# The last two units of each output layer taken one token half at a time, with short chains moved and given priority

## The chip, the cores and the metric

The kernel runs on one core of one Trainium2 chip. The metric is the device time of one execution in microseconds (us), the median of several runs. Five compute engines work side by side, each on its own queue of instructions in a fixed order: PE (TensorE) multiplies matrices and transposes, DVE (VectorE) and ACT (ScalarE) do elementwise work and read the PSUM banks that PE fills, POOL (GpSimd) does a little elementwise work, SP (SyncE) issues DMAs. An instruction that waits holds up everything behind it on its own engine.

## The reference

One token sequence (256 tokens of width 1024, fp32) passes through two blocks of a language model. A matrix product is written `@`:

```
first block : x += rms(rwkv_and_conv(rms(x)) @ w_out) * g1      ("wout")
              x += rms(memory_attention(rms(x)) @ wo) * g3      ("wo")
              x += rms(swiglu(rms(x))) * g5                     (FFN wgu, wdn)
second block: x += swiglu(rms(x))       f1, layer 0
              x += attention(rms(x)) @ wao      (rotary positions, 8 heads)
              x += swiglu(rms(x))       f2, layer 0
              x += swiglu(rms(x))       f1, layer 1
              x += ssm(rms(x)) @ wso            (8 groups of 4 heads)
              x += swiglu(rms(x))       f2, layer 1
swiglu(h) = (silu(h @ Wg) * (h @ Wu)) @ Wd, 2816 = 11 * 256 wide
```

The first three sums normalise the product before it is added to x (the change's texts call this "with post"); the six of the second block add it as it is ("without post").

## The kernel before

**Precision.** Every operand of a large product is split into a high and a low part, and a product is three matmuls: high by high, high by low, low by high. For activations the split comes with the eviction from PSUM: ACT writes the high part, then DVE the low part out of the same bank and the high part (L383 and L384 after a transpose; L301 and L303 elsewhere).

**Weights.** `unit()` brings 1 MB of weights by DMA, ACT casts it in two halves to `wh` (L205, L198), and DVE subtracts to get `wl` (L207, L199); for some units of the SSM stage POOL does this subtraction instead. `wh` and `wl` have four half-unit buffers each, so a cast waits until PE has done with the half four back.

**Products.** An FFN has 11 chunks c: gate and up products of chunk c, four transposes of chunk c-1, and the down product of chunk c-1 into four PSUM banks `acc` (two token halves th by two column halves o). `down_steps` runs a down unit over all four banks; only for the last unit of a layer it goes bank by bank, and `fin.done(th, o)` is called when a bank is complete. The layers wout, wo, wao and wso use the same function.

**Between layers.** `Fin.done` adds the finished bank to x. Without post that is one DVE sum (L414). With post ACT squares the bank and sums (L426), DVE and POOL make the root (L430, L317, L318), and DVE scales and adds (L436, L437). Then `square` sums x squared on ACT (L370) for the next layer's norm, and `PreT.turn(th, q)` transposes four 128x128 blocks of x on PE (L378) and evicts each block by ACT (L383) and DVE (L384): these blocks are the next layer's operand, k = 4q to 4q+3. The next layer's first chunk c0 takes token half 0 through k = 0 to 7 before half 1, so that it needs the turns of half 1 later ("late" turns, taken after an odd k).

**Order.** PE runs in the order in which the program is written. `weave()` mixes a list of generators of large products with short chains, each started at a given step and moved on by what it yields, so that a product step stands between two links of a chain. DVE, ACT and POOL are ordered by a scheduler that goes by readiness and by the priority of the code (`tc.high_priority()`).

**Attention.** `pair(j)` norms and rotates two heads (`rope_norm`, L1176 to L1194), and E0 steps later transposes them (`to_F`, L1201). **SSM.** `steps()` makes the step sizes by a softplus chain of some twenty 128x64 operations (L1339 to L1367, last the tile `adt`). `group(g)` starts every eight steps: ACT turns two banks of broadcast sums into decays (L1440), DVE makes the conv (L1402, L131), masks (L1452), PE mixes, DVE collects y (L1490 to L1493), ACT squares (L1496), POOL takes a power (L1499), DVE multiplies 2 numbers per lane (L1500), ACT scales (L1502), and D2 steps later PE transposes y (L1507).

Of the kernel before, what the change touches and what calls it, by code (L numbers as in the profile page):

```python
# [97 lines left out]
def _build(ctx, nc, tc, a):  # L98
# [176 lines left out]
    def down_steps(acc, u, yf, first, fin=None, every=2):  # L275

        hh, hl = yf()
        if fin is not None:
            for th in range(2):
                for o in range(2):  # L280
                    for k in range(2):
                        down_part(acc, u, hh, hl, th, o, k, first, True)
                    fin.done(th, o)
                    yield
            return
# [77 lines left out]
    class PreT:  # L363
# [8 lines left out]
        def turn(self, xt, th, q):  # L372
# [8 lines left out]
            for i in range(4):  # L381
                k, b = 4 * q + i, bk[:, i * 128:i * 128 + 128]
                S.mul(self.xh[:, k, t], b, pc(gname, gi + k))  # L383
                V.scalar_tensor_tensor(self.xl[:, k, t], b, pc(gname, gi + k), f(self.xh[:, k, t]), MUL, SUB)  # L384
# [7 lines left out]
    class Fin:  # L392
# [10 lines left out]
        def turn(self, th, q):  # L403
            self.nxt.turn(self.xt, th, q)

        def turns(self, *w):
            for th, q in w:
                self.late.append(lambda th=th, q=q: self.turn(th, q))

        def done(self, th, o):  # L410
            xt, c = self.xt, slice(o * 512, o * 512 + 512)
            x, y = xt[:, th, c], flat(self.acc[2 * th + o])
            if self.post is None:
                V.tensor_tensor(x, x, y, ADD)  # L414
# [17 lines left out]
            for o in range(2):  # L432
# [5 lines left out]
                self.nxt.square(th, o, x)  # L438
            self.turns((th, 0), (th, 1))
# [371 lines left out]
    y_c = []  # L811
# [89 lines left out]
    def mem_v_unit(j, u, pool, late):  # L901
        mh_, ml_, rbm, rm = kv["x"]
        bk = bank(pool)
        for k in range(8):
            linT_step(bk, u, mh_, ml_, k)
            if k == 3:
                late.pop(0)()
                late.pop(0)()
# [5 lines left out]
    def wout_units():  # L914
        acc.extend([bank(psa), bank(psa), bank(psa), bank(psf)])
        for j, y in enumerate([y_r[0], *y_c]):
            hl = split(y)
            yield from down_steps(acc, unit(a["wout"][(2, 0, 1)[j]]), lambda: hl, j == 0, None, 1)
# [19 lines left out]
    order.__enter__()  # L938
    yl = split(y_r[1])
    u = unit(a["wout"][3])  # L940
# [4 lines left out]
    run(down_steps(acc, u, lambda: yl, False, fin))  # L945
    mem_v_unit(3, um, psb, fin.late)
    for t in fin.late:
        t()
    mixing.close()
    psa = mkpool("psa", 4, space=PSUM)  # L950

# [60 lines left out]
    def outs_():  # L1012
        acc.extend(new_acc())
        for h in range(4):
            u = unit(a["wo"][h], True)
            if h == 3:
                nf.extend(two("wgu", 0)())
                fins.append(Fin(xt, acc, nxt2, "g3r"))
            yield from down_steps(acc, u, lambda: oh[h], h == 0, fins[0] if h == 3 else None)

    fill = [first_heads()]
    for h in (2, 3):
        fill.append(pieces(lambda h=h: unit(a["wq"][h], True), qb[h]))
    fill.append(outs_())
    weave(fill, [(8, mem_head(0)), (9, mem_head(1)), (11, mem_head(2)), (15, mem_head(3))])

    def rope_tables():
# [39 lines left out]
        tab = {}  # L1067
        for n in ("qn", "kn"):
# [6 lines left out]
            tab[n] = (cg, sg_)  # L1075
        return tab


    def ffn(wgu, wd, l, pre, nf, late, nxt, post=None, ahead=None):

        acc = new_acc()
        late = list(late)
        while len(late) > 2:
            late.pop(0)()
# [18 lines left out]

        for c in range(11):
            us = nf if c == 0 else (unit(a[wgu][l * 22 + 2 * c], True, ahead=True), unit(a[wgu][l * 22 + 2 * c + 1], True))
            b = bank(), bank()
            if c in (0, 10):
                for th in range(2):
                    for k in range(8):
                        wide_step(b, us, xh, xl, k, (th,))  # L1110
                        if k % 2 and late:
                            late.pop(0)()
                        if c and th == 0 and k == 5:
                            hl = turned(c - 1)
                    if c == 0 and th == 0:
# [6 lines left out]
            else:  # L1122
# [4 lines left out]
                for th in range(2):  # L1127
                    evict(c, b[th], th)
            d = unit(a[wd][l * 11 + c], True)
            if c:  # L1130
                for i, _ in enumerate(down_steps(acc, pend, lambda: hl, c == 1)):
                    if c == 10 and i == 1:
                        hl10 = turned(10)
            pend = d
        nf = ahead() if ahead else None
        fin = Fin(xt, acc, nxt, post)
        run(down_steps(acc, pend, lambda: hl10, False, fin))
        return nf, fin.late

    rope = rope_tables()  # L1140
    pre, late = nxt2, fins[0].late
    nx = PreT("f1", 0)
    nf, late = ffn("wgu", "wdn", 0, pre, nf, late, nx, "g5r", two("f1gu", 0))
    pre, nx = nx, PreT("mx", 0)
    nf, late = ffn("f1gu", "f1d", 0, pre, nf, late, nx, None,
# [7 lines left out]
    late_ = list(late)  # L1153
# [16 lines left out]
    def rope_norm(bks, n):  # L1170
        r, r2 = norm
        ss = small(8)
        s4 = ss.rearrange("p (h q) -> p h q", h=2)
        for h, bk in enumerate(bks):
            sq = s2("n")
            S.activation(sq, bk, AF.Square)  # L1176
            V.tensor_reduce(s4[:, h], v3(sq), AX.X, ADD)
        V.tensor_tensor(s4, s4, blast(r2, 4), MUL)
        V.tensor_scalar(ss, ss, 1.0 / 128, 1e-6, MUL, ADD)
# [454 lines left out]
```

## Time and profile before

| | |
|---|---|
| median of 3 runs (range) | 1663.1 us (1663.08 to 1664.25) |
| the profiled execution | 1663.16 us |
| its span in the trace | 1661.1 us |
| busy: PE, DVE, ACT, POOL | 1600.0, 1058.9, 864.0, 142.9 us |
| mean TensorE clock granted | 0.987 of full |

The span is what lies between the first and the last instruction; some 2.1 us of the time lie around it. PE is busy for 96% of the span. The clock is granted at one of two levels, 2.4 GHz (1.00 in the rows) or 1.2 GHz; a row of a window gives the mean over the window. All busy times are of this one execution.

### The profile page before, as it was taken

The numbers are of one execution on the slowest core, as the hardware profiler recorded it, in microseconds if no ns is written. First come the engines' busy times: TensorE is split into PE (matmuls) and PEld (weight loads), VectorE is DVE, ScalarE is ACT, GpSimd is POOL, SyncE is SP. The second block draws the span as 40 slices with busy tenths as digits, with TensorE's granted clock in tenths as the row PEclk, the third lists the DMA queues.
The fourth block names the chain that finished last, engine by engine and source line by source line (L and its number), as shares of the span: only waits on it lengthen the run. The fifth ranks groups of instructions, "written<-read, shape, count | busy, mean of one in ns | idle before, by whom it ended". The sixth has DMA issues, their size and how long they took to land.

```text
span 1661.1 us, 21983 instructions
## 1 busy us (share of the span) xinstructions
PE 1600.0 (96%) x8702; PEld 1376.1 (83%) x8702; DVE 1058.9 (64%) x1652; ACT 864.0 (52%) x1432; POOL 142.9 (9%) x154
## 2 busy tenths in 40 slices
PE   8999998989999999999999999999999999999999
PEld 7898988878887888877778887888889889778887
DVE  6888855574545554567665556555559999665453
ACT  6734445563445444456664445444456766564442
POOL 2322200000000000000000000000014333000000
PEclk9999999989999999999999999999999999999999
DMA  7321234445454445452345554554533323455451
GB/s 280 133 76 53 88 131 149 150 147 213 165 217 157 159 181 200 172 193 92 140 191 200 179 193 175 188 201 170 195 121 129 151 102 127 150 206 194 186 188 66
DMA packets 39848, 265.99 MB, mean 160 GB/s; under 512 B 4673, under 2 KB 5441, under 8 KB 8385
## 3 DMA queue, kind: packets, MB, share of 16 engines
q1 hardware_dynamic: 39456, 263.41, 43.0%
q8 instruction: 68, 1.11, 0.3%
q10 hardware_dynamic: 288, 1.18, 0.2%
q14 instruction: 36, 0.29, 0.1%
HBM read 263.52 MB, written 1.05 MB: 159 GB/s over the span
## 4 chain that ended last, share of the span: by engine, by line
PE 77%; DVE 13%; ACT 6%; issue 3%; POOL 1%; DMA 0%; SPq 0%; POOLq 0%; ACTq 0%; DVEq 0%
PE bk L181 74%; DVE wl L207 3%; PE bk L1101 1%; ACT wh L205 1%; DVE s2w L1427 1%; DVE cv L131 1%; DVE s2w L131 1%; DVE sm L1500 1%; ACT s2w L1405 1%; ACT s2w L1440 1%; PE bk L740 1%; ACT s2n L370 0%; PE bk L378 0%; ACT s L383 0%; DVE s2w L436 0%
## 5 line engine op out<-in xcount | busy, mean ns | idle before, releaser
L181 PE MATMUL bk<-wh,s 128*128 128x512 f32 (+1 forms) x2400 | 735.6, 381 | 10.2 <-DVE s L384 4.8
L207 DVE TENSOR_TENSOR wl<-raw,wh 128x1024 fp32r<-128x1024 f32 x344 | 420.2, 1227 | 266.0 <-ACT wh L205 264.3
L205 ACT CAST wh<-raw 128x1024 fp32r<-128x1024 f32 x366 | 382.0, 1049 | 291.2 <-PE bk L181 278.9
L181 PEld LDWEIGHTS bk<-wh,s 128*128 128x128 f32 x2400 | 441.3, 190 | 94.4 <-DVE s L384 8.2
L181 PE MATMUL bk<-wl,s 128*128 128x512 f32 (+1 forms) x1200 | 449.8, 375 | 0.0
L181 PE MATMUL bk<-wh,s2f 128*128 128x512 f32 x1072 | 344.6, 392 | 0.0
L181 PEld LDWEIGHTS bk<-wl,s 128*128 128x128 f32 x1200 | 228.0, 190 | 37.0
L181 PEld LDWEIGHTS bk<-wh,s2f 128*128 128x128 f32 x1072 | 201.3, 188 | 41.6 <-issue 0.2
L181 PE MATMUL bk<-s,wh 128*128 128x256 f32 x1120 | 220.2, 296 | 8.7 <-ACT wh L528 5.9
L181 PE MATMUL bk<-wl,s2f 128*128 128x512 f32 x536 | 208.6, 389 | 0.0
L181 PEld LDWEIGHTS bk<-s,wh 128*128 128x128 f32 x1120 | 180.7, 197 | 12.8 <-ACT wh L528 5.9
L199 DVE TENSOR_TENSOR wl<-raw,wh 128x1024 fp32r<-128x1024 f32 x120 | 144.4, 1221 | 66.1 <-ACT wh L198 66.1
L181 PE MATMUL bk<-s,wl 128*128 128x256 f32 x560 | 160.3, 289 | 0.5 <-DVE wl L529 0.4
L198 ACT CAST wh<-raw 128x1024 fp32r<-128x1024 f32 x120 | 123.0, 1051 | 60.2 <-DMA raw<-f1gu 20.6
L303 DVE TENSOR_TENSOR s2f<-bk,s2f 128x512 fp32r<-128x512 f32 x59 | 40.8, 691 | 134.0 <-ACT s2f L301 133.9
L301 ACT CAST s2f<-bk 128x512 fp32r<-128x512 f32 x59 | 34.6, 586 | 171.2 <-PE bk L1101 168.9
L181 PEld LDWEIGHTS bk<-wl,s2f 128*128 128x128 f32 x536 | 100.7, 188 | 20.4
L181 PEld LDWEIGHTS bk<-s,wl 128*128 128x128 f32 x560 | 110.3, 197 | 1.3 <-DVE wl L529 0.9
L318 POOL TENSOR_TENSOR sm<-sm,mh 128x2 f32<-128x2 f32 (+1 forms) x17 | 17.1, 1003 | 775.0 <-DVE sm L317 346.8
L1094 ACT ACTIVATE s2w<-bk,sm 128x256 f32<-128x256 f32 x110 | 50.6, 472 | 36.2 <-PE bk L181 35.7
L1095 DVE SCALAR_TENSOR_TENSOR s2w<-bk,sm,s2w 128x256 f32<-128x256 f32 x110 | 51.9, 482 | 18.6 <-ACT s2w L1094 18.3
L207 POOL TENSOR_TENSOR wl<-raw,wh 128x1024 fp32r<-128x1024 f32 x22 | 54.9, 2499 | 68.3 <-ACT wh L205 68.2
(327 smaller groups left out, 1426.5 us busy)
## 6 DMA issues: line engine op xcount, KB each, us to landing
raw<-f1gu SPq DMA_DIRECT2D x44, 1024.0 KB, 4.8
raw<-f2gu SPq DMA_DIRECT2D x44, 1024.0 KB, 4.8
raw<-wgu SPq DMA_DIRECT2D x22, 1024.0 KB, 4.8
raw<-f1d SPq DMA_DIRECT2D x22, 1024.0 KB, 4.8
raw<-f2d SPq DMA_DIRECT2D x22, 1024.0 KB, 5.2
raw<-wxbc SPq DMA_DIRECT2D x16, 1024.0 KB, 4.8
raw<-wdn SPq DMA_DIRECT2D x11, 1024.0 KB, 6.4
raw<-win SPq DMA_DIRECT2D x10, 1024.0 KB, 4.8
```

The source lines that it names most:

```text
L131: V.scalar_tensor_tensor(o, src, w, o, MUL, ADD)
L181: PE.matmul(out, lhsT, rhs, start=start, stop=stop, skip_group_check=True)
L198: S.copy(h[:, c], r[:, c])
L199: V.tensor_tensor(l[:, c], r[:, c], f(h[:, c]), SUB)
L205: S.copy(h, r[:, c])
L207: (eng or V).tensor_tensor(l, r[:, c], f(h), SUB)
L301: S.copy(hh, src)
L303: V.tensor_tensor(hl, src, f(hh), SUB)
L318: G.tensor_tensor(r, r, mh[:, 0:n], POW)
L740: PE.transpose(bx[:, u], Z[:, u], ident)
L1094: S.activation(t, b[:, 0], AF.Silu, scale=r[:, th:th + 1])
L1095: V.scalar_tensor_tensor(t, b[:, 1], ru[:, th:th + 1], t, MUL, MUL)
```

## The change

- `down_two` is new: the last two units u and v of each output layer run u half 0, v half 0, u half 1, v half 1. The sum into x (and with post the chain before it) of half 0 comes after v half 0. Without post the two turns of half 0 stand between u half 1 and v half 1; with post they stand inside v half 1.
- The sum, and the evictions in `turn`, run at high priority; `square` moves from the sum to the end of `turn`.
- In an FFN the gate and up units of chunk 10 are requested one chunk earlier, and chunk 10 is transposed in two halves (`turned_last`).
- `rope_tables` runs inside the `wo` layer's weave instead of after it.
- `rope_norm` and the softplus chain run at high priority; E0 goes from 5 to 7, D2 from 9 to 11; `group` yields `1 + pr` in place of 1, `weigh` yields 7 or 8 in place of 3 or 4 for the last two.
- The multiply at L1500 moves from DVE to POOL.

```diff
+    def down_two(acc, u, yu, v, yv, fin):
+        for th in range(2):
+            hh, hl = yu(th)
+            for o in range(2):
+                for k in range(2):
+                    down_part(acc, u, hh, hl, th, o, k, False, False)
+            yield
+            if th and fin.post is None:
+                fin.turn(0, 0)
+                fin.turn(0, 1)
+            hh, hl = yv(th)
+            for o in range(2):
+                for k in range(2):
+                    down_part(acc, v, hh, hl, th, o, k, False, True)
+                fin.done(th, o)
+                if th and fin.post is not None:
+                    fin.turn(0, o)
+                yield
...
+            with tc.high_priority():
+                for i in range(4):
+                    k, b = 4 * q + i, bk[:, i * 128:i * 128 + 128]
+                    S.mul(self.xh[:, k, t], b, pc(gname, gi + k))
+                    V.scalar_tensor_tensor(self.xl[:, k, t], b, pc(gname, gi + k), f(self.xh[:, k, t]), MUL, SUB)
+            self.square(th, q, xt[:, th, q * 512:q * 512 + 512])
...
         def done(self, th, o):
+            with tc.high_priority():
+                self.update(th, o)
+            if th:
+                self.late.append(lambda: self.turn(1, o))
...
-            yield 1
+            yield 1 + pr
...
-        V.tensor_tensor(rs, rs, rh, MUL)
+        G.tensor_tensor(rs, rs, rh, MUL)
...
-    D0, D1, D2 = 2, 5, 9
+    D0, D1, D2 = 2, 5, 11
...
-    E0, E1, E2 = 5, 3, 6
+    E0, E1, E2 = 7, 3, 6
```

Two places show how the order moves. The first is ACT at the boundary from FFN f2 of layer 0 to f1 of layer 1. Before: `bk_8694` holds blocks k = 0 to 3 of token half 0 and `bk_8716` blocks 4 to 7, `wh_8824` and `wh_8828` are the halves of the first down unit of the next FFN.

```order
L383 ACTIVATE s8_8692<-bk_8694,pk_121 128x128 [waits PE_49]
L370 ACTIVATE s2n_8690,sm_7375<-s8_2753 128x512 [waits DVE_49]
L383 ACTIVATE s8_8692<-bk_8694,pk_121 128x128 [waits DVE_49]
L205 CAST wh_8824<-raw_8822 128x1024 [waits DMAHW1_49,PE_49,Activation_49]
L383 ACTIVATE s8_8692<-bk_8694,pk_121 128x128 [waits DVE_49]
L370 ACTIVATE s2n_8714,sm_7375<-s8_2753 128x512 [waits DVE_49]
L383 ACTIVATE s8_8692<-bk_8716,pk_121 128x128 [waits PE_49]
L205 CAST wh_8828<-raw_8822 128x1024 [waits Activation_49]
L383 ACTIVATE s8_8692<-bk_8694,pk_121 128x128 [waits DVE_49]
```

Now the same place: `bk_8690` holds blocks 0 to 3, `bk_8705` blocks 4 to 7, `bk_8747` the late turn (1, 0); `wh_8833` and `wh_8837` are the down unit's halves.

```order
L397 ACTIVATE s8_8688<-bk_8690,pk_121 128x128 [waits PE_49]
L397 ACTIVATE s8_8688<-bk_8705,pk_121 128x128 [waits PE_49]
L205 CAST wh_8833<-raw_8831 128x1024 [waits DMAHW1_49,PE_49,Activation_49]
L397 ACTIVATE s8_8688<-bk_8705,pk_121 128x128 [waits DVE_49]
L397 ACTIVATE s8_8688<-bk_8690,pk_121 128x128 [waits DVE_49]
L383 ACTIVATE s2n_8760,sm_7377<-s8_2715 128x512
L397 ACTIVATE s8_8688<-bk_8705,pk_121 128x128 [waits DVE_49]
L383 ACTIVATE s2n_8781,sm_7377<-s8_2715 128x512
L397 ACTIVATE s8_8688<-bk_8690,pk_121 128x128 [waits DVE_49]
L397 ACTIVATE s8_8688<-bk_8747,pk_121 128x128 [waits PE_49]
L205 CAST wh_8837<-raw_8831 128x1024 [waits Activation_49]
```

The two banks of half 0 are now evicted in turns, and the cast that waits for PE stands in front of block 1 (it stood in front of block 2); block 3, the next of `bk_8690`, follows two rows after the end of this piece. The second place is POOL in one group of the SSM stage. Before: `wl` is a weight subtraction, `s1v` an input of the group's own mixing product, `sm` the 128x2 power (L1499).

```order
L1401 MEMSET s2n_11661 128x2x3
L207 TENSOR_TENSOR wl_11680<-raw_11676,wh_11678 128x1024 [waits DMAHW0_49,PE_49,Activation_49]
L1499 TENSOR_TENSOR sm_11525<-sm_11525,mh_117 128x2 [waits DVE_49,Activation_49]
L207 TENSOR_TENSOR wl_11684<-raw_11676,wh_11682 128x1024 [waits PE_49,Activation_49]
L1472 TENSOR_TENSOR s1v_11623<-s2w_11617,dec0_10692 128x256 [waits DVE_49]
```

Now the same group; L1527 is the multiply that stood on DVE as L1500.

```order
L1428 MEMSET s2n_11673 128x2x3
L207 TENSOR_TENSOR wl_11692<-raw_11688,wh_11690 128x1024 [waits DMAHW0_49,PE_49,Activation_49]
L207 TENSOR_TENSOR wl_11696<-raw_11688,wh_11694 128x1024 [waits PE_49,Activation_49]
L1526 TENSOR_TENSOR sm_11558<-sm_11558,mh_117 128x2 [waits DVE_49,Activation_49]
L1527 TENSOR_TENSOR sm_11558<-sm_11558,rh_10720 128x2 [waits Pool_49]
L1499 TENSOR_TENSOR s1v_11647<-s2w_11641,dec0_10704 128x256 [waits DVE_49]
```

Both weight subtractions now stand ahead of the power, one behind the other, and the multiply has joined POOL's queue.

## Rows read from the trace of the kernel before

**Rows 1.** The waits of PE over the span: what waited, for which instruction, us in total, times, the longest.

```profile
PE bk L181 <- ACT s2w L1440: 11.8, 7, 2.0
PE bk L181 <- DVE s L384: 6.6, 7, 1.8
...
PE bk L181 <- ACT s L383: 5.7, 9, 1.6
PE bk L1201 <- DVE s2w L1194: 5.6, 2, 4.0
...
PE bk L181 <- DVE adt L1367: 2.4, 1, 2.4
```

**Rows 2.** Busy time of each engine in stretches of the span: us, then PE, PEld, DVE, ACT, POOL busy (instructions), the granted clock, the DMA share, GB/s. In this order: around the end of wout, of wo and of the first FFN (two each), the attention, the boundary between f2 and f1, the SSM start (two), and one SSM group, from the matmul behind one long wait to that behind the next.

```profile
260.00:270.00 10.00, 7.19 (x58) 6.57 (x57) 8.76 (x14) 8.24 (x20) 0.55 (x1) 1.00 0.48 173
270.00:280.00 10.00, 7.61 (x40) 7.28 (x41) 4.86 (x19) 3.94 (x14) 0.70 (x1) 0.66 0.39 128
330.00:340.00 10.00, 8.05 (x38) 6.09 (x36) 6.63 (x10) 6.31 (x14) 0.54 (x1) 1.00 0.51 201
340.00:350.00 10.00, 7.70 (x21) 5.45 (x22) 7.83 (x27) 6.29 (x17) 0.54 (x1) 0.51 0.45 157
530.00:540.00 10.00, 5.75 (x24) 3.38 (x22) 8.35 (x16) 8.04 (x19) 1.08 (x2) 0.91 0.52 188
540.00:550.00 10.00, 9.75 (x37) 7.98 (x38) 7.07 (x21) 5.16 (x18) 0.70 (x1) 0.75 0.34 129
790.00:800.00 10.00, 5.99 (x26) 4.75 (x25) 8.68 (x26) 6.09 (x18) 1.64 (x1) 0.88 0.58 210
1031.00:1041.00 10.00, 9.20 (x45) 7.07 (x44) 9.74 (x23) 8.92 (x22) 1.69 (x1) 1.00 0.35 137
1260.00:1270.00 10.00, 7.55 (x58) 7.15 (x56) 9.93 (x21) 5.13 (x8) 5.70 (x3) 0.93 0.36 116
1270.00:1280.00 10.00, 10.00 (x63) 9.48 (x64) 9.14 (x14) 6.81 (x11) 2.46 (x1) 0.73 0.53 200
1323.18:1341.43 18.25, 16.24 (x131) 15.59 (x131) 16.81 (x31) 12.13 (x29) 6.12 (x5) 1.00 0.30 114
```

**Rows 3.** PE in order of time at the start of a layer: start, us, what, and in brackets the idle time before it and its releaser. First the boundary from f2 to f1, then the end of the first FFN.

```profile
1031.07 0.60 PE L378 MATMUL bk<-idt,s 128*128 128x128 f32 x4
1031.42 0.48 PE L181 MATMUL bk<-wh,s 128*128 128x512 f32 x1
...
1035.72 0.50 PE L181 MATMUL bk<-wh,s 128*128 128x512 f32 x1 [0.52 <-DVE s L384]
...
1036.97 0.62 PE L181 MATMUL bk<-wh,s 128*128 128x512 f32 x2
1037.43 0.40 PE L181 MATMUL bk<-wl,s 128*128 128x512 f32 x1
...
533.69 1.23 PE L378 MATMUL bk<-idt,s 128*128 128x128 f32 x8 [1.26 <-DVE s L437]
```

**Rows 4.** ACT and DVE in order of time around the f2 to f1 boundary, with the first row of the next layer's eviction (L1094).

```profile
1031.04 1.04 ACT L205 CAST wh<-raw 128x1024 fp32r<-128x1024 f32 x1
1031.98 0.37 ACT L383 ACTIVATE s<-bk,pk 128x128 fp32r<-128x128 f32 x1
1032.24 0.62 ACT L370 ACTIVATE s2n<-s 128x512 f32<-128x512 f32 x1
...
1032.85 0.36 ACT L383 ACTIVATE s<-bk,pk 128x128 fp32r<-128x128 f32 x1
...
1039.51 0.47 ACT L1094 ACTIVATE s2w<-bk,sm 128x256 f32<-128x256 f32 x1 [0.42 <-PE bk L181]
...
1032.11 1.23 DVE L207 TENSOR_TENSOR wl<-raw,wh 128x1024 fp32r<-128x1024 f32 x1
1033.25 0.60 DVE L384 SCALAR_TENSOR_TENSOR s<-bk,pk,s 128x128 fp32r<-128x128 f32 x2
```

**Rows 5.** ACT at the end of the first chunk behind the first FFN: the second eviction of c0.

```profile
553.98 0.47 ACT L1094 ACTIVATE s2w<-bk,sm 128x256 f32<-128x256 f32 x1
```

**Rows 6.** One SSM group: POOL, DVE, ACT and PE in order of time.

```profile
1331.23 0.70 POOL L1499 TENSOR_TENSOR sm<-sm,mh 128x2 f32<-128x2 f32 x1 [4.03 <-DVE sm L1498]
1331.90 2.40 POOL L207 TENSOR_TENSOR wl<-raw,wh 128x1024 fp32r<-128x1024 f32 x1
...
1331.97 2.35 DVE L1500 TENSOR_TENSOR sm<-sm,rh 128x2 f32<-128x2 f32 x1 [0.49 <-POOL sm L1499]
...
1340.26 1.12 ACT L1440 ACTIVATE s2w<-bk,acT 128x128 f32<-128x128 f32 x4
...
1341.43 0.50 PE L181 MATMUL bk<-ahl,ohr 128*128 128x256 f32 x2 [2.01 <-ACT s2w L1440]
```

**Rows 7.** DVE between 1290 and 1430 us by line: count, busy us, mean ns, idle time before and what ended it.

```profile
L1427 DVE SCALAR_TENSOR_TENSOR s2w<-s2n,s2w 128x512 f32<-128x512 f32 x8 | 16.1, 2008 | 2.1 <-ACT s2n L1426 2.0
L1500 DVE TENSOR_TENSOR sm<-sm,rh 128x2 f32<-128x2 f32 x7 | 14.3, 2040 | 3.8 <-POOL sm L1499 3.8
```

**Rows 8.** DVE near the end of the softplus chain, and PE's instruction that waits for it.

```profile
1256.91 0.68 DVE L1402 TENSOR_TENSOR s2n<-bk,s1k 128x512 f32<-128x512 f32 x1
...
1263.64 2.43 DVE L1359 TENSOR_SCALAR sm<-sm 128x64 f32<-128x64 f32 x1
...
1269.10 1.06 PE L181 MATMUL bk<-adt,s2y 128*128 128x64 f32 x4 [2.42 <-DVE adt L1367]
```

More of the change, by code (lines that the diff above doesn't have):

```diff
@@ L273, in down_part, with down_steps @@
         mm(bk, hl[:, k, t], h, False, last and k == 1)
-    def down_steps(acc, u, yf, first, fin=None, every=2):
-        hh, hl = yf()
[L278 to L285, printed above, removed]
+    def down_two(acc, u, yu, v, yv, fin):
[16 more added lines that the diff above has]
+                yield
+    def down_steps(acc, u, yf, first, every=2):
+        hh, hl = yf()
         n = 0
@@ L938, in _build @@
     order.__enter__()
+    yc = split(y_c[1])
     yl = split(y_r[1])
-    u = unit(a["wout"][3])
+    u, v = unit(a["wout"][1]), unit(a["wout"][3])
     um = unit(a["wkv"][7])
@@ L944, in _build, with outs_of @@
     fin = Fin(xt, acc, nxt, "g1r")
-    run(down_steps(acc, u, lambda: yl, False, fin))
+    run(down_two(acc, u, lambda th: yc, v, lambda th: yl, fin))
     mem_v_unit(3, um, psb, fin.late)
-    for t in fin.late:
-        t()
     mixing.close()
     psa = mkpool("psa", 4, space=PSUM)
+    def outs_of(n, l, get, nfs, nx, fins, nxt, post, acc):
+        acc.extend(new_acc())
+        for g in range(l - 2):
+            yield from down_steps(acc, unit(a[n][g], True), lambda: get[g], g == 0)
+        u, v = unit(a[n][l - 2], True), unit(a[n][l - 1], True)
+        nfs.extend(two(*nx)())
+        fins.append(Fin(xt, acc, nxt, post))
+        yield from down_two(acc, u, lambda th: get[l - 2], v, lambda th: get[l - 1], fins[0])
     def two(n, l):
@@ L1010, in _build @@
     fins = []
[L1012 to L1025, printed above, removed]
+    rope = {}
     def rope_tables():
@@ L1102, in turned, with turned_last, gate_up @@
             return split(bk, "f")
+        last = []
+        def turned_last(th):
+            if not last:
+                last.extend((s2("f", F32R), s2("f", F32R)))
+            bk, t = bank(), slice(th * 128, th * 128 + 128)
+            for i in range(2):
+                PE.transpose(bk[:, i, 0:128], ts[10][:, th, i * 128:i * 128 + 128], ident)
+            with tc.high_priority():
+                split(bk[:, :, 0:128], "f", last[0][:, :, t], last[1][:, :, t])
+        def gate_up(c):
+            return unit(a[wgu][l * 22 + 2 * c], True, ahead=True), unit(a[wgu][l * 22 + 2 * c + 1], True)
+        us10 = None
         for c in range(11):
-            us = nf if c == 0 else (unit(a[wgu][l * 22 + 2 * c], True, ahead=True), unit(a[wgu][l * 22 + 2 * c + 1], True))
+            us = nf if c == 0 else us10 or gate_up(c)
             b = bank(), bank()
@@ L1265, in _build @@
     nx2 = PreT("f2", 0)
-    def outs_():
-        acc.extend(new_acc())
-        for j in range(4):
-            u = unit(a["wao"][j], True)
-            if j == 3:
-                nf2.extend(two("f2gu", 0)())
-                fins.append(Fin(xt, acc, nx2))
-            yield from down_steps(acc, u, lambda: ao[j], j == 0, fins[0] if j == 3 else None)
     fill = [wide(lambda: nf, qk[0], late_, True)]
@@ L1297, in _build @@
     V.tensor_copy(ohr, C("oneh"))
-    for t in late:
+    for t in fin.late:
         t()
```

206 lines of the change are left out of this document (98 added, 108 removed).

## The prediction

> **What bounds the kernel now.** I read the busy shares first: PE is busy for 1600 of the 1661.1 us of the span, so what can be won are PE's gaps and the stretches at half clock that stand behind them. The waits of PE [rows 1] say which gaps there are: ACT's decays in the SSM groups (11.8 us in seven waits of about 2), the evictions at the starts of layers (L384 6.6, L383 5.7), the rotated heads of the attention (5.6 in two) and the end of the softplus chain (2.4). The windows [rows 2] give what a gap costs with its clock. Around the end of the first FFN PE is idle for 4.25 + 0.25 = 4.5 us, and the clock of 0.91 and 0.75 takes 0.9 + 2.5 = 3.4 more; around wo it is 1.95 + 2.3 = 4.25 and 4.9, around wout 2.8 + 2.4 = 5.2 and 3.4. At the boundary from f2 to f1 only 0.8 us are idle and the clock stays at 1.00. PE's work itself does not change: the matmuls and transposes are the same, in another order.
>
> **1. Attention: 6.8 us off.** PE waits twice for `rope_norm`'s last sum, 1.6 and 4.0 us [rows 1], and the window of the long wait has a clock of 0.88, which is 1.2 us [rows 2]. E0 puts two more steps of the weave between the chain and its transposes; a step is six matmuls at 0.23 us, half the distance between 1036.97 and 1037.43 [rows 3], so two steps are 2.8 us. That covers the short wait and leaves 1.2 of the long one, which priority takes: DVE no longer runs a weight subtraction in front of the chain (1.14 us, from 1032.11 to 1033.25) [rows 4]. All goes: 5.6 + 1.2 = 6.8. The bounds are 4 (a new wait for weights that now come late) and 6.8.
>
> **2. Softplus: 5.8 us off.** PE waits 2.42 us for `adt` at 1269.10, and the chain's small operation at 1263.64 took 2.43 us [rows 8]. At high priority the chain runs nearly unbroken and in the new order ends a few rows behind the second conv sum, which DVE reached at 1256.91 [rows 8]; that is some 8 us before the need. The clock behind the wait, 0.93 and 0.73 [rows 2], is 0.7 + 2.7. What is late next is the conv's own work, which is only needed by later groups. Bounds 2.4 (the clock falls all the same) and 5.8.
>
> **3. SSM groups: 5 us off.** Of the two DVE operations that take 2.0 us in the mean [rows 7], the multiply of 2 numbers is one: it ran from 1331.97 to 1334.32 while POOL subtracted weights from 1331.90 to 1334.30 [rows 6]. So the multiply itself does not cost that; it stood behind POOL. ACT's decays came late by this (1340.26 for a bank filled at 1335), and PE waited 2.01 us [rows 6]. With the multiply on POOL the next DVE operation takes the block, if POOL is still at its subtraction. And the new order puts both subtractions (2.4 us each) behind one another on POOL while DVE collects y. A group takes 18.25 us, of them PE 16.24 and DVE 16.81 [rows 2]. Without its two blocks (2.35 for 0.16, and about 2.45 for 0.69) DVE's work is 12.85; with both subtractions in the way (about 4.5) and the wait for the conv's tanh (some 0.7, an estimate) I come to 18.0 a group. The first two or three groups run without the gap, until DVE's lateness, which may grow to some 4 us now that `bo` is what waits for the bank, is used up; then a gap of nearly 2 us is back. That is 2 to 3 gaps of 2.0 less, 5 us. Bounds 0 and 14 (all seven groups at PE's own work: 7 x 2.0).
>
> The Trainium skill says of this ("SBUF — State Buffer", Who interferes with whom) that a VectorE instruction with two SBUF inputs contends with a GpSimd instruction that reads SBUF, and that whichever starts first holds the shared port for its whole instruction. The rows above agree. It speaks against the move of the multiply: by this rule the block passes to the next sum of two SBUF tiles, and the term is the 5 us; without it the term would be the 14.
>
> **4. The three ends with post: 5.5 us off.** At the end of the first FFN PE finished its products at 533.69 - 1.26 = 532.43 and then waited for the sum [rows 3]. Now half 0's sum runs under u's and v's second halves and both turns of half 0 are in time: PE is ready with them 0.35 us (a turn) [rows 3] after 532.43. But then ACT has in its queue the square of half 1, a square of x, a cast that waited for v, another square, and two more casts and two squares among the eight blocks of half 0; DVE has the scaling and sum of half 1 (four operations, 2.6 us) and the subtractions. Laid out by their durations the low parts of blocks 1, 2 and 3 arrive some 3, 5.5 and 8 us after the turn; PE stands for 5 of 7 us there, and c0 ends near 550.3 against about 553.3 before (its eviction at 553.98 stood behind a cast) [rows 5]. That is 3 at full clock, and some 1.6 of it goes to the half clock that follows such a stretch at each of these places [rows 2]: 1.3 remain. For wo the same gives 1.7, for wout, whose evictions lie under a memory unit, 2.5. Together 5.5; bounds -3 and 24.6, all that the six windows lost.
>
> **5. The boundaries without post: 11 us on.** These are f1 to attention, wao to f2, f2 to f1, and wso to f2. Count from the moment at which both turns of half 0 are done and PE could start c0 (1031.42) [rows 3]. The cast of the next down unit's first half waits for v, whose first half PE leaves three matmuls (0.7) earlier, so it runs from -0.4 to 0.55 (a cast is 0.94, 1031.04 to 1031.98) [rows 4]. Before, blocks 0 and 1 were out by then; now block 0 and block 4 are, because the two banks are evicted in turns. Block 1 follows at 1.1 us; two squares (0.61 each, 1032.24 to 1032.85) and one block later, block 2 at 2.8; behind a late block, the second cast and two more blocks, block 3 at 4.8 (before: blocks 2 and 3 at about 0.8 and 2.9). DVE's low parts have subtractions of 1.14 between them, so block 3's comes at 6.05, where before PE took it at 1035.72, which is 4.3. Then PE has the second late turn (0.35) and twelve matmuls (2.75): half 0 ends near 9.6 where it ended near 7.8 (the eviction came a little behind it, at 1039.51) [rows 4]. So about 2 us are lost at each, on top of 0.8 that stay. PE's standing time grows from 0.8 to about 3 us within 6; where PE stood that much before, the clock fell [rows 2], and I put 0.7 on each for a fall at some of them (a fall costs 1.7 to 3.4). 4 x 2.7 = 11. Bounds -3.2 (the 0.8 us go at each) and 22 (2 and a long fall each). The boundary into the SSM stage, whose late turns stand at once behind the products, I count at nothing (-1 to 1).
>
> **6. What costs nothing.** `rope_tables` under wo: ACT is busy for 6.31 of 10 us there [rows 2], and PE has products of its own; if it delays the memory softmax, 1 to 2 us. Chunk 10 requested early passes the down unit of chunk 9 on SP's queue, with a chunk (some 17 us) of products as cover; v's second half is cast only after the last gate and up products, about 0.8 us before PE needs its low part, which five FFNs could lose (up to 2). `weigh`'s later yields bring its matmuls between the output layer's own, with 12 matmuls (2.7 us) ahead of their use.
>
> **The sum,** against the profiled execution (1663.16, where the median of the runs is 1663.1): 1663.2 - 6.8 - 5.8 - 5 - 5.5 + 11 = 1651.
>
> **Rivals.**
> (a) The queues at the boundaries do not matter and DVE is freed in the SSM groups: part 5 becomes -3.2 and part 3 -14, so 1651 - 14 - 9 = 1628. For it: PE's waits at the boundaries are now small and the turns come 2.7 us sooner. Against it: the order of ACT, and POOL's two subtractions in a row. 0.12.
> (b) Gains and losses cancel: the attention and the softplus chain give 10, the SSM groups nothing as DVE stays as blocked as it was, the ends with post 2 and the boundaries cost 13: 1662. For it: DVE is busy for over 9 of 10 us in the SSM start [rows 2]. 0.18.
> (c) Slower, by the starts of layers: the early turns of half 0 meet the casts of the next layer's weights on ACT, PE stands for 3 us at each of the four boundaries and the clock falls behind every one as it did at 270 to 280 us (3.4 us there) [rows 2]. That is 4 x (2 + 3.4) = 21.6, the ends with post give nothing for the same reason, and the SSM groups nothing: 1663.2 - 12.6 + 21.6 = 1672. It decides from 3.2 us a boundary on, if parts 3 and 4 give nothing. 0.18.
> The forecast has the rest, 0.52, with its own range of 1643 to 1659.
>
> **How the numbers follow.** A measurement of this kernel tells about 0.2% (3.3 us) from no change, so faster means under 1659.8 and slower over 1666.4. Faster: the forecast and (a), 0.64; same: (b), 0.18; slower: (c), 0.18. The range leaves out the far half of (a) and of (c): 1632 to 1669.
>
> **What would show it.** In the changed profile the two waits for `rope_norm` and the one for `adt` are gone. At the four boundaries PE's waits for the evictions (now L397 and L398) grow to 2 to 3 us each, on block 1 to 3, with a cast on ACT just before; if they are under 0.5, part 5 is wrong. In the SSM groups POOL shows two subtractions in a row, and in each some DVE sum of two SBUF tiles of over 2 us; PE's waits are missing in the first groups and back in the later ones; if they are missing in all, part 3 is too small. If the clock is 1.00 around the three ends with post, part 4 is too small by up to 12.

## The result, and the profile after

The changed kernel takes 1673.3 us (median of 4 runs, 1672.1 to 1674.2), the kernel before 1663.1 beside it: a ratio of 1.006 with a 95% interval of 1.0043 to 1.0078. It is slower, by 10 us. The forecast was 1651 with a range up to 1669, so both the sign and the range were wrong.

The profiled execution took 1672.1 us, with a span of 1670.2. PE is busy for 1605.0 us of it (before 1600), at the same mean clock. To see where the time went I cut both spans at marks that exist in both: PE's first transposes in the mixing (L740 before, L751 after), its first transposes of a chunk's products in each of the five FFNs, and its last instruction. Each number is the difference of two start times on PE's timeline, each rounded to 0.1 us.

| stretch | before, us | after, us | difference |
|---|---|---|---|
| start to the mixing | 80.8 | 79.8 | -1.0 |
| mixing, wout, memory, wo, to the first FFN | 282.9 | 277.8 | -5.1 |
| first FFN, end with post, to f1 | 195.0 | 193.9 | -1.1 |
| f1, attention, wao, to f2 | 303.3 | 306.4 | +3.1 |
| f2 to the second f1 | 188.1 | 191.7 | +3.6 |
| f1, SSM stage, wso, to the last f2 | 438.3 | 447.7 | +9.4 |
| last f2 to the end | 168.4 | 168.4 | 0 |

The ends with post gained 6.2; the boundaries without post and above all the SSM stage lost more. Inside the SSM stretch, up to the first group's transposes (L1462 before, L1489 after) it is 243.7 and 245.7, from the first to the eighth group's 128.3 and 136.0, and the rest 66.3 and 66.0. (The order of PE's work moves these inner marks, by some 0.6 us of work at most.)

The waits of PE after, in the same view as [rows 1]:

```profile
PE bk L181 <- issue: 11.3, 6, 2.1
PE bk L181 <- ACT s L397: 6.7, 15, 0.8
...
PE bk L181 <- DVE s L398: 6.0, 14, 1.2
PE bk L181 <- DVE wl L207: 3.9, 1, 3.9
...
PE bk L181 <- DVE s2f L1541: 2.6, 1, 2.6
PE bk L181 <- DVE s2f L1497: 2.4, 2, 1.4
...
PE bk L181 <- DVE s2c L1485: 2.1, 1, 2.1
PE bk L1277 <- ACT s2f L1270: 2.0, 1, 2.0
```

And one of before that [rows 1] do not show, the sum at the ends with post:

```profile
PE bk L378 <- DVE s L437: 5.9, 5, 1.5
```

The waits for the sum at the ends with post (5.9; one of 0.6 is left), the rotated heads (5.6) and `adt` (2.4) are gone. In the place of the last two stand others: the transposes of a head's softmax, which wait for ACT's scaling (L1277 for L1270, 2.0), and a weight's low part (3.9). The line of the decays (11.8) is gone by name only. In the SSM groups the view has six waits marked "issue" (11.3: five of about 2 us, one of 0.9), all before the product into the bank `bo` (`bk<-s1v,s2o`). Each ends 0.10 us after ACT's fourth row of decays out of a bank (L1467). ACT, then PE:

```profile
1322.98 1.11 ACT L1467 ACTIVATE s2w<-bk,acT 128x128 f32<-128x128 f32 x4
...
1324.19 0.67 PE L181 MATMUL bk<-s1v,s2o 128*128 128x256 f32 x2 [1.97 <-issue]
```

So by the times it is the old wait, for a bank that ACT is still reading, at another product; the view names no releaser. What is new in the groups are waits for DVE's results (2.6, 2.4 and 2.1) and for a low part from POOL (1.3). The evictions (L397, L398) are as long in sum as L383 and L384 were, but in 29 waits, not 16. The windows, with the columns of [rows 2], show three places where a wait and a fall of the clock come together, and two SSM groups:

```profile
520.00:530.00 10.00, 9.37 (x43) 6.69 (x41) 7.76 (x16) 7.97 (x19) 1.08 (x2) 1.00 0.36 129
530.00:540.00 10.00, 8.01 (x22) 5.41 (x23) 7.72 (x16) 5.25 (x14) 1.54 (x1) 0.66 0.57 206
540.00:550.00 10.00, 10.00 (x48) 8.28 (x47) 7.74 (x13) 6.80 (x13) 0.00 (x0) 1.00 0.21 71
...
1027.00:1037.00 10.00, 8.30 (x28) 5.20 (x27) 9.11 (x22) 8.38 (x20) 1.51 (x1) 0.83 0.58 211
1255.00:1265.00 10.00, 6.09 (x48) 5.89 (x48) 9.73 (x33) 6.79 (x10) 0.30 (x3) 0.87 0.26 103
...
1344.11:1363.87 19.76, 17.66 (x131) 17.22 (x131) 16.86 (x30) 12.06 (x29) 6.45 (x6) 0.91 0.30 106
...
1383.63:1403.41 19.78, 16.27 (x131) 15.80 (x131) 16.88 (x30) 12.01 (x29) 6.46 (x6) 1.00 0.31 108
```

Around 530 us PE's idle time fell from 4.25 + 0.25 = 4.5 to 0.63 + 1.99 = 2.6, but the clock costs the 3.4 us that it did before, now in one window of 0.66. At the boundary from f2 to f1, where the clock was 1.00, it is 0.83 and 1.7 us are idle. The group takes 19.76 us instead of 18.25, with DVE's busy time unchanged (16.86 and 16.81). It is not the clock that makes it longer: at 0.91 and at 1.00 a group takes the same time.

**One SSM group after.** POOL, DVE and ACT in order of time:

```profile
1347.60 4.92 POOL L207 TENSOR_TENSOR wl<-raw,wh 128x1024 fp32r<-128x1024 f32 x2 [10.69 <-ACT wh L205]
1355.87 0.20 POOL L1527 TENSOR_TENSOR sm<-sm,rh 128x2 f32<-128x2 f32 x1
...
1347.83 2.46 DVE L1519 TENSOR_TENSOR s2f<-s2f,s1v 128x256 f32<-128x256 f32 x1
1350.32 2.76 DVE L1520 TENSOR_TENSOR s2f<-s2f,s2c 128x512 f32<-128x512 f32 x1
...
1358.35 0.48 DVE L1541 SCALAR_TENSOR_TENSOR s<-bk,pk,s 128x256 fp32r<-128x256 f32 x1 [2.06 <-ACT s L1540]
...
1353.11 0.42 ACT L1523 ACTIVATE s2c<-s2f 128x256 f32<-128x256 f32 x1 [4.57 <-DVE s2f L1520]
...
1356.10 0.91 ACT L1529 ACTIVATE s2f<-s2f,sm 128x256 f32<-128x256 f32 x2 [1.19 <-POOL sm L1527]
1356.92 1.03 ACT L205 CAST wh<-raw 128x1024 fp32r<-128x1024 f32 x1
1357.85 0.46 ACT L1540 ACTIVATE s<-bk,pk 128x256 fp32r<-128x256 f32 x1
```

POOL's two subtractions run back to back for 4.92 us, and DVE's two operations for y that start meanwhile, a sum and a product (both are called sums below), take 2.46 and 2.76 (0.42 and 0.69 in groups without it, below). ACT idles 4.57 for y, then squares it; POOL makes the two numbers; ACT scales y, casts a weight for 1.03, and only then evicts (L1540) what DVE's L1541 waits for. DVE idles 2.06 there. 16.86 busy, 2.06 here and 0.73 for the conv's tanh make 19.65 of the 19.76 us.

**The softplus chain after.** POOL, then DVE, then ACT, then PE:

```profile
1249.72 3.27 POOL L207 TENSOR_TENSOR wl<-raw,wh 128x1024 fp32r<-128x1024 f32 x1 [0.81 <-ACT wh L205]
...
1250.64 2.39 DVE L1373 TENSOR_SCALAR sm<-sm 128x64 f32<-128x64 f32 x1
...
1261.29 0.22 DVE L1394 TENSOR_TENSOR adt<-dt,na 128x64 f32<-128x64 f32 x1
1261.42 1.67 DVE L131 SCALAR_TENSOR_TENSOR s2w<-s2n,pk,s2w 128x256 f32<-128x256 f32 x4
1263.00 1.23 DVE L207 TENSOR_TENSOR wl<-raw,wh 128x1024 fp32r<-128x1024 f32 x1
...
1255.97 1.98 ACT L205 CAST wh<-raw 128x1024 fp32r<-128x1024 f32 x2
...
1264.28 0.58 PE L181 MATMUL bk<-s,wl 128*128 128x256 f32 x1 [3.91 <-DVE wl L207]
```

`adt` comes at 1261.5, in time. But the chain and the conv's sums around it kept the weight subtraction, whose cast ACT had made by 1257.0, waiting until 1263.00; PE, idle from 1260.37, took that low part at 1264.28.

### The profile page after: what moved, and what is told of

It is laid out like the page before. It is cut to its first block, busy times and chain, and to the rows that moved or that the text cites. A ratio compares the mean times of both kernels' runs of the same rounds, so it can differ in the third digit from the quotient of the medians.

```text
span 1670.2 us, 21978 instructions
## 1 busy us (share of the span) xinstructions
PE 1605.0 (96%) x8702; PEld 1374.4 (82%) x8702; DVE 1062.8 (64%) x1649; ACT 864.9 (52%) x1437; POOL 148.5 (9%) x162
## 4 chain that ended last, share of the span: by engine, by line
PE 74%; DVE 14%; ACT 6%; issue 3%; POOL 1%; DMA 0%; SPq 0%; POOLq 0%; DVEq 0%; ACTq 0%
PE bk L181 71%; DVE wl L207 3%; DVE s2w L131 2%; ACT wh L205 2%; PE bk L1111 1%; DVE cv L131 1%; ACT s2w L1467 1%; DVE s2f L1519 1%; DVE s2f L1520 1%; ACT s L397 1%; PE bk L751 1%; PE bk L391 1%; DVE s2n L1429 1%; ACT s2w L1432 0%; DVE s L398 0%
## 5 line engine op out<-in xcount | busy, mean ns | idle before, releaser
L181 PE MATMUL bk<-wh,s 128*128 128x512 f32 (+1 forms) x2400 | 745.0, 384 | 14.7 <-ACT s L397 6.1
L314 ACT CAST s2f<-bk 128x512 fp32r<-128x512 f32 (+1 forms) x64 | 35.3, 552 | 167.8 <-PE bk L1111 161.4
L316 DVE TENSOR_TENSOR s2f<-bk,s2f 128x512 fp32r<-128x512 f32 (+1 forms) x64 | 41.5, 649 | 126.2 <-ACT s2f L314 126.1
```

The lines of the kernel that those rows point to most:

```text
L181: PE.matmul(out, lhsT, rhs, start=start, stop=stop, skip_group_check=True)
L314: S.copy(hh, src)
L316: V.tensor_tensor(hl, src, f(hh), SUB)
```

## The experiments

Each run is the changed kernel with the edit shown (e9: the kernel before), timed in three or more rounds beside the kernel before, which took 1662.8 to 1663.3 us on those chips. All compute the whole reference. "SSM stretch" is the sixth row of the table. Two notes on noise: the head up to the mixing varied from 79.7 to 83.3 us between the profiles of kernels that are equal there, and the f2 to f1 stretch from 190.0 to 191.7. So I read differences under 3 us from the stretches, not from the times.

**e1: the three edits in the SSM groups undone together.**

```diff
-            yield 1 + pr
+            yield 1
...
-        G.tensor_tensor(rs, rs, rh, MUL)
+        V.tensor_tensor(rs, rs, rh, MUL)
...
-    D0, D1, D2 = 2, 5, 11
+    D0, D1, D2 = 2, 5, 9
```

> The changed kernel with the three edits of the SSM groups undone (the pair yields 1 again, D2 is 9, the multiply of 128x2 numbers is on DVE). Theory: the new order of the groups costs the most, since their period grew from 18.2 to 19.7 us; then this run is 9 to 11 us faster than the changed kernel (1662 to 1664) and PE's gap is again 2.0 us a group in a period of 18.2. Rival: the groups are slow because DVE comes into them late from the softplus chain and the boundary before; then the period stays above 19 and the run wins under 3 us.

1670.1 us (1669.8 to 1671.2), ratio 1.004 (1.0025 to 1.0055): only 3.2 less, against an expectation of 9 to 11. The eight groups are back at 127.8 us, and the waits for the decays have their old name again (9.3 us in six). But the rest of the stage is 70.2 us instead of 66.0, so the SSM stretch is only 4.0 shorter; the clock is 0.92, 0.91 and 0.87 at 1290 to 1310 and 1480 to 1490 us, where the changed kernel has 1.00, which is some 3 us. The groups are the largest loss, but these edits undone give back only about half of it over the stage.

**e2: the softplus chain without priority and in its old order.** (The `with tc.high_priority():` ahead of it is taken out.)

> The changed kernel with the softplus chain at normal priority. Theory: the chain's priority only exchanged one wait for another (2.4 us for adt before, 3.9 us for a weight subtraction now); then the wait for weights goes, that for adt of 2 to 3 us comes back, and the time is within 2 us of the changed kernel (1671 to 1675). Rival: the priority does harm by the subtractions it pushes back; then the run is 3 to 6 us faster.

1674.0 us (1671.7 to 1676.4), ratio 1.0058 (1.0041 to 1.0075). PE waits 2.4 us for `adt` again, and the wait of 3.9 for the low part is gone. The stretch to the first group is 2.1 us shorter, the SSM stretch 0.9: one wait had been exchanged for another.

**e3: the boundaries without post undone.** `down_two` runs one unit after the other there:

```diff
+        if fin.post is None:
+            yield from down_steps(acc, u, lambda: yu(0), False)
+            yu(1)
+            hh, hl = yv(0)
...
+            return
```

> The changed kernel with the layers without post as before: u over all four banks, then v bank by bank, the turns of half 0 inside v's second half. Theory: each of the boundaries into an FFN costs 3 to 3.6 us in the changed kernel (measured at f2 to f1: 3.6), as the evictions of half 0 meet the casts of the next weights on ACT; then this run is 10 to 14 us faster (1659 to 1663) and the waits at the four boundaries are 0.8 us again. Rival: the loss lies in the SSM stage alone; then it wins under 4 us.

1666.8 us (1665.6 to 1667.6, 10 runs), ratio 1.0021 (1.0011 to 1.003): 6.5 less than the changed kernel, where I had expected 10 to 14. The stretches: f1 to f2 302.4 (-4.0), f2 to f1 188.9 (-2.8), SSM stretch 446.2 (-1.5), 8.3 in sum. At the f2 to f1 boundary PE waits 0.57 and 0.53 only. Part of this is the clock. In e5, e7 and e8 below, whose kernels are the changed one up to there, PE stands as long at that boundary (8.30 us busy) and the clock stays at 1.00; in e8:

```profile
1028.80:1038.80 10.00, 8.30 (x35) 5.31 (x34) 9.53 (x23) 8.32 (x20) 1.51 (x1) 1.00 0.56 211
```

Beside e8 the same edit (e10 below) is worth 2.5, 1.3 and 1.5 in the three stretches, 5.3 in sum.

**e4: the attention's edits undone.**

```diff
-        yield 7 + j % 2 if j // 2 else 3 + j % 2
+        yield 3 + j % 2
...
-    E0, E1, E2 = 7, 3, 6
+    E0, E1, E2 = 5, 3, 6
```

(and `rope_norm` without its two `with tc.high_priority():`)

> The changed kernel with rope_norm at normal priority, E0 5 and the old yields of weigh. Theory: the attention's edits are worth the two waits of 1.6 and 4.0 us less the new wait of 2.0, with their clock; then this run is 3 to 6 us slower than the changed kernel (1676 to 1679), with the waits for rope_norm back. Rival: the gain was eaten by the new wait and its clock; then it is within 2 us of it.

1678.5 us (1677.6 to 1680.7), ratio 1.0092 (1.0077 to 1.0107): 5.3 more. Both waits for the rotated heads are back (5.6, longest 4.0); the f1 to f2 stretch is 3.5 longer. The wait at the softmax's transposes is gone with the edits, so it is their price. This part of the change gains.

**e5, e6, e7: the three edits of e1, one at a time.** e5 takes the multiply to DVE, e6 sets D2 to 9, e7 is `yield 1`.

> The changed kernel with only the multiply of 128x2 numbers back on DVE. Theory: where this multiply runs is not what makes the group 19.7 us long, since POOL's two subtractions block the next sums of DVE with or without it; then the time is within 1.5 us of the changed kernel (1672 to 1675) and DVE still shows two sums of about 2.5 us in each group. Rival: POOL's queue (the multiply and the product behind it) delays y and with it the whole chain; then it is 3 us faster or more.

> The changed kernel with only D2 back to 9. Theory: D2 = 11 put the eviction of y's transposes (ACT L1540, DVE L1541) behind the scaling of the next group's y on ACT, and DVE stands 2.06 us a group there (1356.3 to 1358.35 in the changed kernel's trace); then this wait goes, the period falls from 19.7 to between 18 and 18.7 us, and the run is 5 to 9 us faster. Rival: the two blocks by POOL set the period alone; then it stays at 19 us or more and the run wins under 3 us.

> The changed kernel with only the pair's yield back to 1, which on POOL puts the power and the multiply between the two weight subtractions again. Theory: DVE's two blocks in a row (L1519 and L1520, 2.46 and 2.76 us) become one there and one elsewhere, y is done some 2.4 us sooner, and the period falls to 18 to 18.7 us; the run is 5 to 9 us faster. Rival: the blocks only change their place and DVE's wait for ACT stays; then it wins under 3 us.

e5 took 1665.4 us (1658.5 to 1667.1, 10 runs), ratio 1.0012 (1.0003 to 1.0022), 7.9 less; e6 1676.8 (1675.2 to 1678.6), ratio 1.0084 (1.0069 to 1.0099), 3.5 more; e7 1659.3 (1654.6 to 1660.9, 8 runs), ratio 0.9972 (0.9962 to 0.9983), 14 less. My expectation fell in all three. In e6 its rival held as to the period: the groups stay at 136.2 us. The parts don't add either: -7.9, +3.5 and -14 make -18, and all together gave -3.2. In e5 POOL still holds up the same two sums; what changed is ACT's and DVE's order behind them:

```profile
1346.17 2.47 DVE L1519 TENSOR_TENSOR s2f<-s2f,s1v 128x256 f32<-128x256 f32 x1
...
1355.78 0.47 DVE L1541 SCALAR_TENSOR_TENSOR s<-bk,pk,s 128x256 fp32r<-128x256 f32 x1
...
1353.16 1.05 ACT L205 CAST wh<-raw 128x1024 fp32r<-128x1024 f32 x1
1354.45 0.91 ACT L1529 ACTIVATE s2f<-s2f,sm 128x256 f32<-128x256 f32 x2 [0.24 <-DVE sm L1527]
1355.27 0.45 ACT L1540 ACTIVATE s<-bk,pk 128x256 fp32r<-128x256 f32 x1
```

The cast now lies ahead of L1529, under POOL's power, and L1540 follows L1529 directly; DVE has no idle time at L1541, and the groups come every 18.1 us. A group of the changed kernel takes 1.7 us more, near its idle time of 2.06. In e7 POOL's two subtractions lie apart, with the power and the multiply between them (POOL, then DVE):

```profile
1342.18 2.40 POOL L207 TENSOR_TENSOR wl<-raw,wh 128x1024 fp32r<-128x1024 f32 x1 [6.81 <-ACT wh L205]
...
1349.59 2.40 POOL L207 TENSOR_TENSOR wl<-raw,wh 128x1024 fp32r<-128x1024 f32 x1
...
1342.66 2.47 DVE L1454 SCALAR_TENSOR_TENSOR s2w<-s2n,s2w 128x512 f32<-128x512 f32 x1
...
1345.50 0.42 DVE L1519 TENSOR_TENSOR s2f<-s2f,s1v 128x256 f32<-128x256 f32 x1
1345.96 0.69 DVE L1520 TENSOR_TENSOR s2f<-s2f,s2c 128x512 f32<-128x512 f32 x1
1351.34 0.48 DVE L1541 SCALAR_TENSOR_TENSOR s<-bk,pk,s 128x256 fp32r<-128x256 f32 x1 [2.49 <-ACT s L1540]
```

One sum (L1454) is held up; the other subtraction falls into the 2.49 us that DVE stands for ACT anyway. A group takes 17.2 us.

**e8: POOL's weight subtractions of the SSM groups on DVE.**

```diff
-        fill.append(pieces(lambda g=g: unit(a["wz"][g], True, eng=G), bzs[g], True))
+        fill.append(pieces(lambda g=g: unit(a["wz"][g], True), bzs[g], True))
```

> The changed kernel with the weight subtractions of the units wz on DVE in place of POOL, so that POOL blocks nothing in a group. Theory: DVE then has 12.85 us of its own and 2.3 of subtractions and no block of 2 x 2.0; the period falls to 16.3 to 17.5 us, and the run is 11 to 20 us faster than the changed kernel (1653 to 1662). Rival: the chain from y over ACT and POOL back to DVE sets the period, whatever blocks; then it stays above 18.5 us and the run wins under 7 us.

1648.4 us (1644.2 to 1650.8), ratio 0.9911 (0.9895 to 0.9926): 25 less, beyond what I had expected. DVE takes on two subtractions of 1.22 a group, and is busy for less:

```profile
1344.00:1359.75 15.75, 15.75 (x131) 15.45 (x130) 14.18 (x29) 12.16 (x28) 1.82 (x5) 1.00 0.41 139
```

PE has no gap in the group at all.

**e9: the same edit in the kernel before.**

> The kernel before, with one edit: the wz weights' low parts are subtracted on DVE instead of POOL. My theory now: it is POOL's two subtractions of a group that cost, in either kernel, since each holds up one of DVE's sums; the same edit in the changed kernel took its group period from 19.8 to 15.75 us. Here the period should go from 18.25 to about 16.3 us, PE's seven waits for the decays of about 2.0 us go, and the time falls by 10 to 16, to some 1647 to 1653. Rival: DVE, busy 16.8 of 18.25 us already, becomes the bound once it takes 2 x 1.15 us more a group: period 18 or above, time 1660 to 1668.

1644.4 us (1643.6 to 1645.6), ratio 0.989 (0.9875 to 0.9905): the theory holds, and the gain of 18.4 is above its range. The lines of DVE that [rows 7] show at 2008 and 2040 ns now have 683 and 161:

```profile
L1427 DVE SCALAR_TENSOR_TENSOR s2w<-s2n,s2w 128x512 f32<-128x512 f32 x8 | 5.5, 683 | 0.0
L1500 DVE TENSOR_TENSOR sm<-sm,rh 128x2 f32<-128x2 f32 x8 | 1.3, 161 | 4.4 <-POOL sm L1499 4.4
```

**e10 and e11: what the runs point to.** e10 is e3 and e8 together; e11 also takes the odd conv weights from POOL:

```diff
-        fill.append(pieces(lambda i=i: unit(a["wxbc"][8 + i], True, eng=(V, G)[i % 2]), bc[i]))
+        fill.append(pieces(lambda i=i: unit(a["wxbc"][8 + i], True), bc[i]))
```

> The changed kernel with two edits: the four output layers without post go back to one unit after the other, and the wz weights' low parts are subtracted on DVE. Each alone gave 6.5 and 25 us. They lie in different stages, so theory: they add, 1673.3 - 31 = 1642, range 1638 to 1646. Rival: a common resource (the weight buffers or SP's queue) carries the SSM gain over into the last boundary, and the sum is under 27: over 1646.

> The run with both edits, and a third: the odd wxbc weights too have their low parts subtracted on DVE, so that POOL subtracts no weights in the SSM stage at all. Theory: DVE's held-up operations at the softplus stage (3.0 us twice and 2.4 in the chain) go, and with them the wait of 3.9 us for a weight's low part and the clock behind it: 4 to 7 us less than the run with two edits, some 1636. Rival: DVE was full there (over 9 of 10 us), and each subtraction it takes over (1.15 us) comes late by as much as the hold-up was: within 2 us of it, or slower.

e10 took 1642.1 us (1641.5 to 1646.0), ratio 0.988 (0.9866 to 0.9895): 31 less than the changed kernel, so the two gains add. e11 took 1636.9 (1636.4 to 1637.4), ratio 0.9844 (0.9829 to 0.9859), the fastest of all and 26 under the kernel before. Most of that is not the change's: with the wz subtractions on DVE in both, the changed kernel (e8, 1648.4) is still 4.0 slower than the one before (e9, 1644.4), and e10 only 2.3 faster. The kernel before with both of POOL's streams on DVE was not run. The window of e11 where the changed kernel stood 3.9 us for a low part:

```profile
1255.00:1265.00 10.00, 10.00 (x84) 9.76 (x83) 10.00 (x25) 6.98 (x11) 0.10 (x1) 1.00 0.44 151
```

DVE is full there with two more subtractions, and PE doesn't stand at all.

**e12: `yield 1` and the multiply on DVE, D2 left at 11.**

> The changed kernel with both halves of a pair's memory step one step apart again (yield 1) and the multiply of the two numbers on DVE; D2 stays 11. The runs so far: yield 1 alone gave -14.0, the multiply alone -7.9, D2 = 9 alone +3.5, all three -3.2. If the effects are separate, this one is -14 -8 = -22, 1651. Theory now: they are not separate, both only cure the same loop (which DVE sum is held up by which subtraction), so this one is about as the yield alone, 1656 to 1663, and D2 = 9 accounts for the rest of the difference to -3.2 (some 8 to 11, a wait of PE for a decay copy in the tail). Rival: the multiply on DVE with yield 1 is itself bad (it is behind a subtraction again, as before), and D2 = 9 costs nothing: 1668 to 1671.

1672.4 us (1671.7 to 1676.0), ratio 1.0063 (1.0046 to 1.008): its rival was right (1668 to 1671, a little exceeded), and it is 13 us slower than e7. The multiply on DVE starts just behind a subtraction again (POOL, then DVE):

```profile
1354.22 2.41 POOL L207 TENSOR_TENSOR wl<-raw,wh 128x1024 fp32r<-128x1024 f32 x1
...
1354.28 2.35 DVE L1527 TENSOR_TENSOR sm<-sm,rh 128x2 f32<-128x2 f32 x1 [0.87 <-POOL sm L1526]
```

So D2 is not what kept e1 slow, and the sum of e5 and e7 is not to be had. In e5 no subtraction follows the power, in e7 the multiply is on POOL itself; only with both edits does it start on DVE just behind a subtraction.

## Why the prediction was wrong

**Part 3, the SSM groups: -5 forecast, +7.7 measured. This is the step that failed.** The reading that POOL's two subtractions come in a row and hold up two sums was right, and so were the terms of DVE's work: I had 12.85 + 4.5 + 0.7 = 18.05 for a group, and DVE was busy for 16.86 and idle for 0.73. Wrong was to take this sum for the period, as if ACT always had DVE's next operand ready. y's sums, held up, release ACT's squares, these POOL's power and multiply, these ACT's scaling, then a cast, then the eviction that DVE needs next. This loop gives the 2.06 us of idle time that no term held; and of the "2 to 3 gaps" that were to go, one went (seven waits of PE to six). e5, without it, has the period of 18.1 that I forecast; its eight groups take 126.6 us against 128.3 before. So even there the gain is 1.7 and not 5: that the first groups would run without a gap was wrong as well, by some 3 us, and the multiply on POOL, with the loop behind it, cost the other 9.4 (136.0 less 126.6).

The Trainium skill's rule ("SBUF — State Buffer", Who interferes with whom), that a VectorE operation with two SBUF inputs and a GpSimd operation that reads SBUF exclude each other and the first to issue holds the port, agrees with these runs: 2.35 for a multiply of two numbers that alone takes 0.16, and no sum lengthened in the groups of e8 and e9 (0.42 and 0.69 for y). As told here it does not cover the 2.39 of L1373 in the softplus chain, which reads one SBUF tile only (its like, L1386, takes 0.20). I had used it to price one operation. What it was worth was the opposite question, which I didn't ask: what the group takes if POOL subtracts no weights. That gave 18 to 25 us.

**Part 2, the softplus chain: -5.8 forecast, +2.0 measured (243.7 to 245.7 up to the first group), outside its bounds too.** This is the second step that failed. The wait for `adt` went, as forecast. "What is late next is the conv's own work, which is only needed by later groups" failed: the chain's priority and POOL's two hold-ups of DVE (3.0 for two sums, 2.39 for the chain's own small operation) delayed a weight's low part, and the new wait (3.9) is longer than the old (2.4), with the clock at 0.87 and 0.79 around it. I had costed what the priority moves ahead, and not what stands behind it on a full engine; e11 shows that DVE without POOL has room for both: there the stretch is 238.4 us, 5.3 under the kernel before.

**Part 5, the boundaries without post: +11 forecast, 5.3 to 8.3 measured.** The mechanism is as forecast. PE, then ACT, at the f2 to f1 boundary:

```profile
1027.39 0.39 PE L181 MATMUL bk<-wh,s 128*128 128x512 f32 x1
...
1030.31 0.50 PE L181 MATMUL bk<-wh,s 128*128 128x512 f32 x1 [0.31 <-ACT s L397]
...
1032.29 0.50 PE L181 MATMUL bk<-wh,s 128*128 128x512 f32 x1 [0.57 <-ACT s L397]
...
1033.54 0.68 PE L181 MATMUL bk<-wh,s 128*128 128x512 f32 x1 [0.53 <-DVE s L398]
...
1026.95 1.05 ACT L205 CAST wh<-raw 128x1024 fp32r<-128x1024 f32 x1 [1.09 <-issue]
...
1028.42 0.62 ACT L383 ACTIVATE s2n<-s 128x512 f32<-128x512 f32 x1
...
1029.28 0.63 ACT L383 ACTIVATE s2n<-s 128x512 f32<-128x512 f32 x1
...
1030.39 1.06 ACT L205 CAST wh<-raw 128x1024 fp32r<-128x1024 f32 x1
```

A cast, two squares and another cast lie between the eight evictions, and PE takes block 3's low part at 1033.54, 6.15 us after c0's first matmul (1027.39); I had laid it out at 6.05. The size is over: PE stands 1.7 us in that window where I had 3 for the whole start, and the loss is 2.8 here, 4.0 for two boundaries and 1.5 for wso; without the clock's fall, from e8 to e10, it is 1.3, 2.5 and 1.5. (The end of half 0, 9.6 in my text, is 9.15 by its own terms, as 7.8 is 7.4; the difference of about 2 stands.) e3 shows what the order costs as a whole; moving only the squares or only the casts was not tried.

**Part 4, the ends with post: -5.5 forecast.** The profile has -6.2 (5.1 and 1.1 in the table). In the other runs, equal up to there, the first of the two stretches took 279.0 to 281.4 us, a gain of 1.5 to 3.9, and both together gained 2.2 to 5.4. So the mechanism holds, and the size was near the top of what was measured. In the first stretch PE's idle time hardly differs between these runs (12.4 to 12.9 us); what differs is the clock, which costs 3.4 us in the profile of the changed kernel and 5.1 to 6.8 in the others. My upper bound of 24.6 should have been 25.7 by the six windows. At 530 us the clock does fall behind the shorter waits, as I had allowed for with 1.6 of the 3 us.

**Part 1, the attention: -6.8 forecast, -3.5 by the stretch and -5.3 by the time of e4.** Both waits went, and a new one came, of the softmax's transposes for ACT (L1277, 2.0 us). My bound of 4 allowed for a new wait, but for weights.

**Rivals and sum.** (c) had the right side and nearly the right time (1672), but at the wrong place: it put 21.6 on the boundaries and nothing on the SSM groups, where +7.7 lay. So its time was luck. (The terms of (b) make 1664, not 1662.) No rival had the groups slower than before; the bounds of part 3 were 0 to 14 of gain, those of part 2 2.4 to 5.8. That is where the range failed: parts 2 and 3 together came 20.5 us above the forecast, of 22 in all, and either of them alone as forecast would have left the time under 1669. Of the +3.1 from f1 to f2, the boundaries and the attention explain +0.5, and 2.6 stay open. (In e5, e7 and e8, equal there, the stretch takes 305.0: the clock costs 1.7 us instead of 3.4; e3 has that gain in its 4.0 as well.) Of the six waits of PE marked as issue one is left in e8, of 0.9 us.

## What to carry to other kernels

Where two engines hold each other up, try first what the time is with one of the two streams taken off altogether; an operation moved out of the way can pass the hold-up to the next one in the queue. A period is the longest loop through all engines, not the busy time of the fullest: add up who waits for whom around one repeat, idle times included. And price a priority by what stands behind it on a full engine.

## What the runs showed of the hardware

POOL's weight subtractions were a loss here: one of 1024 columns takes 2.40 us on POOL and 1.22 on DVE, and where one on POOL met a sum of DVE, it held DVE for 1.8 to 2.2 us more than the sum needs. In e7 one of the two met none, as DVE was standing. With both of a group's subtractions taken over, DVE's busy time in a group fell from 16.86 to 14.18 us. The hold-up goes the other way too: the subtraction at 1249.72 took 3.27 us on POOL, as DVE's own had started just before it, at 1249.51 (1.22).

The same idle time does not always bring the clock down: at the f2 to f1 boundary PE was busy for 8.30 of 10 us in the changed kernel and in e8, and the clock was 0.83 in one and 1.00 in the other.

At the end of the first FFN PE stood for 2.6 us in four gaps of 0.3 to 1.0 where it had stood for 4.5 in gaps of up to 1.6, and the clock still fell behind them, to 0.66 of full speed over 10 us (which is 6.8 us at the lower level, 1.2 GHz). The shorter waits saved at most their own 1.9 us (the stretch gained 1.1) and nothing of the clock.
